# Tile starts at multiples of 64 bytes, deeper buffers in stick-breaking and up-projection, and an output projection begun by contraction block

## The chip, the core and the metric

The kernel runs on one core of one Trainium2 chip. The metric is the device time of one execution in microseconds (us). Times of before are from three runs; a further execution was profiled, and all rows below are of that one.

## What is computed

One decoder layer over 1024 tokens of width 1024, float32 throughout. Two attention families run from one input projection, are projected up, gated and summed, and go through an output projection; then a squared-ReLU MLP. Each half has a shift, a scale and a gate computed from a vector `c` ("ada"). Cut to what matters here:

```python
mod = jax.nn.silu(c) @ ada_w + ada_b
shift1, scale1, gate1, shift2, scale2, gate2 = jnp.split(mod, 6, axis=-1)
z = (rms_norm(h, norm1_g) * (1 + scale1) + shift1) @ w_in
...                                   # q_a, k, v of NSA; q_b, k_b, v_b; m_a, m_b
y_a = nsa_attention(...) @ w_up_nsa   # compressed, selected and sliding-window branches
y_b = stick_breaking_attention(q_b, k_b, v_b) @ w_up_sb
mixed = (jax.nn.sigmoid(m_a) * y_a + jax.nn.sigmoid(m_b) * y_b) @ w_out
h = h + gate1 * mixed
u2 = rms_norm(h, norm2_g) * (1 + scale2) + shift2
ff = jnp.square(jax.nn.relu(u2 @ mlp_w1)) @ mlp_w2
return h + gate2 * ff
```

Stick-breaking has no softmax: with z the scaled logits, the weight of a key is sigmoid(z) times the product of sigmoid(-z) over the later keys up to the query.

## The kernel before, in words

**Matmuls.** Every large product is made of three TensorE (PE) passes: each float32 operand is split into a rounded high half and the rest (tiles ending in `h` and `l`, by `hi` and `lo`, lines 57 to 66), and high by high, high by low and low by high are summed in PSUM. A matmul has a stationary operand of 128x128 and a moving one of up to 512 columns.

**Memory.** Tiles are taken from pools that grow from two ends of the on-chip memory, "left" and "right". The right end begins 32 bytes off a multiple of 64, so with tile sizes that are multiples of 64 a right-hand tile starts at 32 modulo 64; odd-sized tiles (`rows`, `zero` of 4 bytes, `Pt` of 513 elements, `wh1`/`wl1` of 536) shift what lies behind them.

**Stages** (times of the profiled execution): norm and first projections (0 to 185; lines 300, 304, 575, 586), native sparse attention (NSA, 215 to 600), stick-breaking (600 to 857), rest of the input projection (to 880), up-projections (880 to 982), output projection (976 to 1092), MLP (1092 to 1756). The columns of `w_in` for q_b, k_b, v_b and the gates are computed as "fill" (line 744, 24 matmuls for one block of 128 columns and 512 tokens): a generator hands out its matmuls between those of the two attentions. `pump` hands out so many us of it at once: 25 ahead of NSA, 20 between NSA and stick-breaking. What is left at the end runs by itself.

**Order.** The code gives each engine's work; a scheduler orders the instructions of each engine when the kernel is built, and each engine runs its list in that order. DMAs are issued from SyncE's (SP's) list, also in order.

**Ada rows.** `ada_rest` (line 410) computes a row of `c @ ada_w` in steps: a load (`adraw`, two buffers), a multiply on ScalarE (ACT, L439), an add on GpSimd (POOL, L443). Row 3 runs in stick-breaking in pieces of 256 columns, row 0 (the gate of the first half) in the up-projection in pieces of 512. `side(n)` runs n steps.

**Stick-breaking** (`sb_gens`). Per head and group: logits on PE (L1121 to L1124) into a bank `psx`, two sigmoids on ACT (L1126 into a tile `sig128` to `sig512` or `sigr`, L1127 in place), a scan on VectorE (DVE, L1136), a product on POOL (L1138), transposes (L1153), a split (`th`, `tl`), and products with V (L1173). At the start, head 0 is prepared: casts and subtractions to `Q`, `Kh`, `Kl` (ACT, POOL), V by transposes and casts (L1091, L1095).

**Up-projection** (lines 1370 to 1397). 16 units (8 blocks of 128 channels, two token halves) for each branch; a unit is 12 matmuls of L1322, a gate tile `m` loaded and put through a sigmoid, and a product (L1379). Branch 1 runs `lag` units behind branch 0 and the two are summed on POOL (L1394) and split to `mth`/`mtl`. Weights come in units of 256 columns (`w_unit`: load into one of three `raw` buffers, cast on POOL L63, rest on DVE L66).

**Output projection** (`out_mm`). The contraction has 8 blocks in four weight units; a result of 128 tokens and 512 columns is 24 matmuls (L1426).

**MLP.** 64 hidden units of 24 matmuls (L1510) alternate with the products of a Strassen-like scheme (L1559, 24 a product).

## Time and profile before

| | us |
|---|---|
| median of 3 runs | 1753.86 |
| lowest, highest | 1750.43, 1757.51 |
| profiled execution | 1757.71 |
| its span in the trace | 1755.7 |
| PE busy in the span | 1697.4 (97%) |
| DVE, POOL, ACT busy | 1140.2, 872.2, 818.1 |

The profiled execution's time lies 2.0 us above its span, which begins with the first instruction and ends with the last. A matmul's duration in the trace is that of its way through the array and overlaps the next; what a matmul costs in a run is the distance from start to start. The granted clock is TensorE's, as a share of 2.4 GHz; the other level is 1.2 GHz.

### The profile page before, as it was taken

To read this page: it belongs to the slowest core of one execution; us is meant where nothing else is said; L and a number is where in the kernel's file an instruction comes from. 1 tells how busy PE (TensorE), PEld (TensorE's weight loads), DVE (VectorE), ACT (ScalarE), POOL (GpSimd) and SP (SyncE) were. 2 spreads that over 40 slices of the span, in tenths; PEclk is the share of its full clock that TensorE was granted. 3 is DMA by queue.
4 is the path that set the end of the run, shared out by engine and by line. 5 is a ranking of instruction groups with operands and counts; after the bars stand their busy time and mean duration, and the time that the engine had idled before them with its cause. 6 is when DMAs were issued, how large, how long until landed. Compare 5 with 4: busy or idle time off the path is not lost.

```text
span 1755.7 us, 25197 instructions
## 1 busy us (share of the span) xinstructions
PE 1697.4 (97%) x8652; PEld 1417.0 (81%) x8652; DVE 1140.2 (65%) x2514; ACT 818.1 (47%) x1809; POOL 872.2 (50%) x824
## 2 busy tenths in 40 slices
PE   5999999999999989999999899999999999999998
PEld 4879888888888867788778687888888888888886
DVE  7597478778777467778454564365656564756458
ACT  6433476666666367766443244333333333333332
POOL 0021143434333387874154400786867675858676
PEclk8999999999999989999999999999999999999999
DMA  9365312112121254531475611121212020202102
GB/s 300 101 191 153 109 46 60 49 54 60 44 59 39 76 156 129 148 84 46 149 249 174 215 37 72 38 71 37 64 41 76 25 72 25 72 25 72 43 19 96
DMA packets 153655, 157.12 MB, mean 89 GB/s; under 512 B 13544, under 2 KB 117688, under 8 KB 153528
## 3 DMA queue, kind: packets, MB, share of 16 engines
q1 hardware_dynamic: 149304, 153.42, 29.3%
q10 hardware_dynamic: 4224, 2.10, 0.4%
q8 instruction: 68, 1.11, 0.3%
q14 instruction: 59, 0.48, 0.1%
HBM read 128.21 MB, written 27.28 MB: 89 GB/s over the span
## 4 chain that ended last, share of the span: by engine, by line
PE 79%; DMA 6%; DVE 4%; POOL 4%; ACT 3%; issue 3%; SPq 1%; POOLq 0%; ACTq 0%; DVEq 0%
PE px L1510 20%; PE px L1559 16%; PE pd L744 15%; PE px L1426 5%; PE po L907 4%; PE pt L941 4%; DMA adraw<-in_ada_w_dram 3%; PE psx L823 2%; PE psx L824 2%; PE po L1173 1%; PE cb L300 1%; PE pd L586 1%; PE psx L586 1%; PE pt L1153 1%; POOL adacc L443 1%
## 5 line engine op out<-in xcount | busy, mean ns | idle before, releaser
L1562 DVE TENSOR_TENSOR acc<-acc,px 128x512 f32<-128x512 f32 x384 | 244.0, 683 | 121.8 <-PE px L1559 116.5
L1510 PE MATMUL px<-mtl,wh 128*128 128x512 f32 x512 | 203.4, 397 | 0.0
L1510 PE MATMUL px<-mth,wl 128*128 128x512 f32 x512 | 203.3, 397 | 0.0
L1510 PE MATMUL px<-mth,wh 128*128 128x512 f32 x512 | 203.0, 397 | 0.0
L744 PE MATMUL pd<-uh,uwh 128*128 128x512 f32 x448 | 180.7, 403 | 0.7 <-ACT zo L1016 0.7
L744 PE MATMUL pd<-ul,uwh 128*128 128x512 f32 x448 | 177.5, 396 | 0.0
L1559 PE MATMUL px<-wbl,rah 128*128 128x512 f32 x448 | 175.5, 392 | 2.1 <-POOL wbl L1535 1.8
L744 PE MATMUL pd<-uh,uwl 128*128 128x512 f32 x448 | 176.9, 395 | 0.0
L1559 PE MATMUL px<-wbh,ral 128*128 128x512 f32 x448 | 174.7, 390 | 0.0
L66 DVE TENSOR_TENSOR wl<-raw,wh 128x1024 fp32r<-128x1024 f32 x48 | 74.9, 1563 | 150.7 <-ACT wh L61 129.2
L1559 PE MATMUL px<-wbh,rah 128*128 128x512 f32 x448 | 172.5, 391 | 0.0
L1535 POOL TENSOR_TENSOR wbl<-raw,wbh 128x1024 fp32r<-128x1024 f32 x40 | 104.2, 2606 | 93.6 <-ACT wbh L1534 93.4
L1521 POOL TENSOR_TENSOR w<-w,grow 128x1024 f32<-128x1024 f32 x32 | 83.1, 2612 | 98.2 <-DVE grow L1294 97.9
L899 DVE TENSOR_TENSOR tl<-pt,th 128x512 fp32r<-128x512 f32 (+8 forms) x168 | 103.7, 620 | 34.5 <-ACT th L898 33.3
L1533 POOL TENSOR_TENSOR raw<-r 128x512 f32<-128x512 f32 x80 | 109.7, 1392 | 20.2 <-DVE wl L66 18.1
L898 ACT CAST th<-pt 128x512 fp32r<-128x512 f32 (+8 forms) x168 | 88.7, 530 | 60.4 <-PE pt L941 58.4
L1510 PEld LDWEIGHTS px<-mth,wl 128*128 128x128 f32 x512 | 96.5, 189 | 23.6 <-DVE grow L1294 0.2
L1510 PEld LDWEIGHTS px<-mtl,wh 128*128 128x128 f32 x512 | 96.6, 189 | 23.2 <-issue 0.2
L1510 PEld LDWEIGHTS px<-mth,wh 128*128 128x128 f32 x512 | 96.6, 189 | 23.1 <-issue 0.2
L1534 ACT CAST rah<-raw 128x1024 fp32r<-128x1024 f32 x40 | 42.0, 1050 | 152.9 <-PE px L1559 139.6
L1559 PEld LDWEIGHTS px<-wbl,rah 128*128 128x128 f32 x448 | 84.1, 188 | 21.4 <-POOL wbl L1535 3.0
L1559 PEld LDWEIGHTS px<-wbh,rah 128*128 128x128 f32 x448 | 84.1, 188 | 18.4
(322 smaller groups left out, 4548.1 us busy)
## 6 DMA issues: line engine op xcount, KB each, us to landing
raw<-in_mlp_w_dram SPq DMA_DIRECT2D x32, 512.0 KB, 4.1
w<-in_mlp_w_dram SPq DMA_DIRECT2D x32, 512.0 KB, 4.1
z_d<-zo SPq DMA_DIRECT2D x56, 256.0 KB, 2.0
uwr<-in_w_in_dram SPq DMA_DIRECT2D x54, 256.0 KB, 3.0
adraw<-in_ada_w_dram SPq DMA_DIRECT2D x48, 256.0 KB, 2.9
xa<-in_ada_w_dram SPq DMA_DIRECT2D x32, 256.0 KB, 6.1
zr<-z_d SPq DMA_DIRECT2D x32, 256.0 KB, 4.8
m<-z_d SPq DMA_DIRECT2D x32, 256.0 KB, 3.3
```

The lines of the kernel that those rows point to most:

```text
L66: (nc.vector if e == "v" else nc.gpsimd).tensor_tensor(dst, src, f(h), op=OP.subtract)
L744: r = nc.tensor.matmul(p, a, b, start=(k == 0 and n == 0), stop=(k == NK - 1 and n == 2))
L898: nc.scalar.copy(th[:rows, :w], p[:rows, :w])
L899: nc.vector.tensor_tensor(tl[:rows, :w], p[:rows, :w], f(th)[:rows, :w], op=OP.subtract)
L907: track(nc.tensor.matmul(po_[:, :256], w, tt[q][:rows, m * 256:(m + 1) * 256], start=(n == 0 and m == 0 and q == 0), stop=(n == last and m ...
L1426: nc.tensor.matmul(p, a[:, k, ts_], b[:, k % 2], start=(k == 0 and n == 0), stop=(k == NK - 1 and n == 2))
L1510: nc.tensor.matmul(p, a[:, k], b[th][:, k], start=(k == 0 and m == 0), stop=(k == NK - 1 and m == 2))
L1521: nc.gpsimd.tensor_tensor(t, t, grow2, op=OP.mult)
L1533: nc.gpsimd.tensor_tensor(d, block(i0, j0, s), block(i1, j1, s), op=OP.add if sg > 0 else OP.subtract)
L1535: (nc.vector if e == "v" else nc.gpsimd).tensor_tensor(l.rearrange("p s n -> p (s n)"), src, f(h).rearrange("p s n -> p (s n)"), op=OP.sub ...
L1559: nc.tensor.matmul(p, a[:, s, qs], b[:, s], start=(s == 0 and n == 0), stop=(s == 1 and n == 2))
L1562: nc.vector.tensor_tensor(acc[:, t, ds_], acc[:, t, ds_], p, op=OP.add if sg > 0 else OP.subtract)
```

## The change

What it does, in the order of the diff:

- A tile of 32 bytes is put first on the right-hand side, and tiles of odd size are made multiples of 64 bytes (`rows` becomes a part of an `acc` tile, 536 columns become 544, 63-column blocks lie in 512 elements, `zero` takes 16 elements, `Pt` 528). `kv_mm` splits its 536 columns 272 and 264 instead of twice 268.
- Stick-breaking: head 0 is prepared on DVE instead of POOL; three `sig` buffers a width instead of two and six `sigr` instead of five; no ada steps in the first three groups; 24 us of fill instead of 20 ahead of it.
- Up-projection: branch 0's gate tiles get seven buffers instead of five, the lag is 5 instead of 3, and ada row 0 goes in pieces of 256 columns, two steps a unit.
- Output projection: the first four results are begun together, 6 matmuls each from one weight unit, before the next unit.

```diff
+    pool("odd", "right").tile([128, 8], F32, name="odd")
     xt_pool = pool("xt", "right")
...
-        rows = xt_pool.tile([72, 128], F32, name="rows")
+        rows = xt_pool.tile([128, 2, 128], F32, name="acc", bufs=2)[:72, 0]
...
-        wh = p1a.tile([128, 536], F32R, name="wh1", bufs=8)
-        wl = p1a.tile([128, 536], F32R, name="wl1", bufs=8)
+        wh = p1a.tile([128, 544], F32R, name="wh1", bufs=8)
+        wl = p1a.tile([128, 544], F32R, name="wl1", bufs=8)
...
-        for c in range(2):
+        for c, (c0, c1) in enumerate(((0, 272), (272, 536))):
...
-        zero = sp.tile([128, 1], F32, name="zero")
+        zero = sp.tile([128, 16], F32, name="zero")[:, 0:1]
...
+            eng, e = (nc.gpsimd, "g") if h else (nc.vector, "v")
...
-            hi(Kh, kr, "g")
+            hi(Kh, kr, e)
             yield
-            nc.gpsimd.tensor_tensor(Q[HD:], qr[HD:], f(Q)[HD:], op=OP.subtract)
+            eng.tensor_tensor(Q[HD:], qr[HD:], f(Q)[HD:], op=OP.subtract)
...
-            lo(Kl, kr, Kh, "g")
+            lo(Kl, kr, Kh, e)
...
-            sig = sp.tile([128, w], F32, name="sigr" if kind == 1 else "sig%d" % w, bufs=5 if kind == 1 else 2)
+            sig = sp.tile([128, w], F32, name="sigr" if kind == 1 else "sig%d" % w, bufs=6 if kind == 1 else 3)
...
-                Pt = sp.tile([128, 513], F32, name="Pt", bufs=6)
+                Pt = sp.tile([128, 528], F32, name="Pt", bufs=6)
...
-                    if c % 2:
+                    if c % 2 and k > 2:
                         side(1)
...
-        m = pool_.tile([128, 512], F32, name="m%d" % br, bufs=5 - 3 * br)
+        m = pool_.tile([128, 512], F32, name="m%d" % br, bufs=7 - 5 * br)
...
-    pump(fill, 20.0)
+    pump(fill, 24.0)
...
-    ada_steps = ada_rest(yb, (0,), 2, "s")
+    ada_steps = ada_rest(yb, (0,), 2, "s", 256)
     side(1)
-    lag = 3
+    lag = 5
...
-        side(1)
+        side(2)
...
+    def out_part(p, t, dh, ks):
         ts_ = slice((t % 4) * 128, (t % 4 + 1) * 128)
         th = t // 4
-        p = px()
-        for k in range(NK):
+        for k in ks:
             wh, wl = wo_s[dh][k // 2]
...
+    def out_mm(t, dh, p=None):
+        ds_ = slice(dh * 512, (dh + 1) * 512)
+        if p is None:
+            p = px()
+            out_part(p, t, dh, range(NK))
...
+    ob_ = [px() for _ in range(4)]
+    for k in range(0, NK, 2):
+        for t in range(4):
+            out_part(ob_[t], t, 0, (k, k + 1))
     for t in range(4):
-        out_mm(t, 0)
+        out_mm(t, 0, ob_[t])
```

Where the operands of the matmuls start, in the two built programs (line numbers of before; bytes modulo 64 of the moving and of the stationary operand, and the difference of the two modulo 256):

| line | what | count | before: moving, stationary | difference | after: moving, stationary | difference |
|---|---|---|---|---|---|---|
| 300 | first blocks | 96 | 0, 32 | 96 | 0, 0 | 64 |
| 304, 575 | q columns | 192 | 0 or 32, 0 | 0, 32, ... 224 | 0, 0 | 0, 128 |
| 744 | fill | 1344 | 0, 0 | 0 | 0, 0 | 0 |
| 907 | NSA, probabilities by V | 592 | 32, 32 | 0 | 0, 0 | 0 |
| 1121, 1122 | stick-breaking logits | 192 | 32, 32 | 0 | 0, 0 | 0 |
| 1322 | branch 0 | 192 | 32, 32 | 0 | 0, 0 | 0 |
| 1322 | branch 1 | 192 | 0, 32 | 96 | 0, 0 | 64 |
| 1426 | output projection | 384 | 32, 0 | 160 | 0, 0 | 192 |
| 1510 | hidden units | 1536 | 0, 32 | 96 | 0, 0 | 64 |
| 1559 | MLP products | 1344 | 0, 0 | 0 | 0, 0 | 0 |

The order of PE at the start of the output projection. Before: `px_12320`, `px_12349` and `px_12378` are the first three results, `wh_12294`, `wh_12300` and `wh_12306` the high halves of weight units 0, 1 and 2.

```order
L1426 MATMUL px_12349<-wl_12301,mth0_11512 128x512
L1426 MATMUL px_12320<-wh_12306,mth0_11512 128x512
L1426 MATMUL px_12349<-wh_12300,mtl0_11514 128x512
L1426 MATMUL px_12349<-wh_12300,mth0_11512 128x512
L1426 MATMUL px_12349<-wl_12301,mth0_11512 128x512
L1426 MATMUL px_12349<-wh_12300,mtl0_11514 128x512
L1426 MATMUL px_12349<-wh_12306,mth0_11512 128x512
```

Unit 2 was first used after 20 matmuls, by the second row above. After, with `px_12390` to `px_12393` the four results, `wh_12364` unit 0 and `wh_12370` unit 1 (the rows where unit 0 gives way to unit 1):

```order
L1427 MATMUL px_12393<-wh_12364,mth0_11516 128x512
L1427 MATMUL px_12393<-wl_12365,mth0_11516 128x512
L1427 MATMUL px_12393<-wh_12364,mtl0_11518 128x512
L1427 MATMUL px_12390<-wh_12370,mth0_11516 128x512
L1427 MATMUL px_12390<-wl_12371,mth0_11516 128x512
```

Unit 1 is first used after 24 matmuls, unit 2 after 48, unit 3 after 72.

The order of POOL around the casts of these weights (L63), among the sums of the two branches (L1394, L1397 after). Before, from the cast of unit 1 to that of unit 3:

```order
L63 TENSOR_SCALAR wh_12300<-raw_12299 128x1024
L1394 TENSOR_TENSOR m1_12107<-m1_12107,m0_11948 128x512
L1394 TENSOR_TENSOR m1_12148<-m1_12148,m0_12002 128x512
L1394 TENSOR_TENSOR m1_12185<-m1_12185,m0_12043 128x512
L1394 TENSOR_TENSOR m1_12208<-m1_12208,m0_12090 128x512
L63 TENSOR_SCALAR wh_12306<-raw_12305 128x1024
L1394 TENSOR_TENSOR m1_12228<-m1_12228,m0_12131 128x512
L63 TENSOR_SCALAR wh_12312<-raw_12311 128x1024
```

After, the same stretch (`wh_12370` is unit 1, `wh_12376` unit 2):

```order
L63 TENSOR_SCALAR wh_12370<-raw_12369 128x1024
L1397 TENSOR_TENSOR m1_12213<-m1_12213,m0_11947 128x512
L1397 TENSOR_TENSOR m1_12238<-m1_12238,m0_12011 128x512
L1397 TENSOR_TENSOR m1_12258<-m1_12258,m0_12057 128x512
L63 TENSOR_SCALAR wh_12376<-raw_12375 128x1024
L1397 TENSOR_TENSOR m1_12278<-m1_12278,m0_12102 128x512
L63 TENSOR_SCALAR wh_12382<-raw_12381 128x1024
L1397 TENSOR_TENSOR m1_12298<-m1_12298,m0_12147 128x512
```

Unit 2's cast has moved ahead of one more branch sum. On SP, the load of unit 0 stood after branch 1's ninth gate tile and ahead of 13 gate tiles; now it stands after branch 0's sixteenth and branch 1's tenth, ahead of 6.

The order of ACT at the start of stick-breaking. Before (`V` casts of head 0 and 1, `adacc` and `adraw` the ada steps):

```order
L439 ACTIVATE adacc<-adraw,cs 128x256
L439 ACTIVATE adraw<-adraw,cs 128x256
L1073 CAST Q<-zr 128x1024
L439 ACTIVATE adraw<-adraw,cs 128x256
L1095 CAST V<-pt 128x4x64 x2
L439 ACTIVATE adraw<-adraw,cs 128x256
L1095 CAST V<-pt 128x4x64 x2
L1126 ACT_TABLE_LOAD
```

After:

```order
L441 ACTIVATE adacc<-adraw,cs 128x256
L1076 CAST Q<-zr 128x1024
L441 ACTIVATE adraw<-adraw,cs 128x256 x4
L1098 CAST V<-pt 128x4x64 x2
L1018 COPY zo<-pd 128x512
L1098 CAST V<-pt 128x4x64 x2
L1129 ACT_TABLE_LOAD
```

Five ada steps instead of four stand ahead of the first sigmoid, and all five ahead of the V casts. Of the fill, 70 matmuls stood between NSA and the first V transpose and now 89; between each twelve products of L1173 it was 18 to 38 throughout, and now it is 12 to 42 with none in the last such stretch.

## Rows read from the trace of the kernel before

**Rows 1.** The page, busy time, share of the span and instructions by engine.

```profile
PE 1697.4 (97%) x8652; PEld 1417.0 (81%) x8652; DVE 1140.2 (65%) x2514; ACT 818.1 (47%) x1809; POOL 872.2 (50%) x824
```

**Rows 2.** Busy time by stretch: engines as its heading says, then clock, DMA share, GB/s.

```profile
core 0: us, PE busy (x) PEld busy (x) DVE busy (x) ACT busy (x) POOL busy (x), PEclk, DMA share, GB/s
...
600.00:640.00 40.00, 33.73 (x155) 27.54 (x154) 16.61 (x33) 17.62 (x37) 23.44 (x23) 0.91 0.69 187
640.00:860.00 220.00, 208.35 (x1130) 172.95 (x1129) 168.79 (x323) 146.83 (x339) 141.26 (x148) 0.98 0.35 93
...
987.00:1026.00 39.00, 39.00 (x163) 31.30 (x163) 22.80 (x36) 8.76 (x20) 8.21 (x6) 0.94 0.62 216
...
1134.00:1710.00 576.00, 576.00 (x2495) 469.39 (x2494) 345.00 (x425) 192.88 (x263) 411.59 (x233) 1.00 0.16 49
```

**Rows 3.** Chain that ended last: start, length in us, engine, tile, line, matmuls.

```profile
45.11 2.83 PE cb L300 x12
...
85.85 5.34 PE qb L575 x23
...
756.60 2.73 PE pd L744 x12
...
856.69 21.80 PE pd L744 x96
...
1030.88 11.22 PE px L1426 x48
...
1133.92 5.46 PE px L1559 x24
1139.39 5.61 PE px L1510 x24
```

**Rows 4.** Timeline of PE in the up-projection, branch 0, then branch 1: start, us.

```profile
882.67 0.39 PE L1322 MATMUL px<-oh,wh 128*128 128x512 f32 x1
...
884.03 0.39 PE L1322 MATMUL px<-oh,wh 128*128 128x512 f32 x1
...
972.08 0.40 PE L1322 MATMUL px<-ol,wh 128*128 128x512 f32 x1
...
974.42 0.39 PE L1322 MATMUL px<-oh,wl 128*128 128x512 f32 x1
```

**Rows 5.** Timeline of PE, its three longest waits after 600 (in brackets).

```profile
631.95 0.47 PE L1121 MATMUL psx<-Kh,Q 128*128 128x128 f32 x1 [5.40 <-DVE Pt L1136]
...
891.67 0.50 PE L1322 MATMUL px<-oh,wh 128*128 128x512 f32 x1 [2.26 <-POOL wh L63]
...
986.08 0.80 PE L1426 MATMUL px<-wh,mth 128*128 128x512 f32 x1 [4.89 <-POOL wh L63]
```

**Rows 6.** Output weights: unit 0's load in the chain, then SP's and POOL's timelines.

```profile
945.87 8.62 DMA raw<-in_w_out_dram
...
956.97 0.38 SPq L1281 DMA_DIRECT2D raw<-in_w_out_dram  x1
...
971.78 0.38 SPq L1281 DMA_DIRECT2D raw<-in_w_out_dram  x1
...
983.75 1.26 POOL L1394 TENSOR_TENSOR m<-m,m 128x512 f32<-128x512 f32 x1 [3.07 <-DVE m L1379]
984.98 1.05 POOL L63 TENSOR_SCALAR wh<-raw 128x1024 fp32r<-128x1024 f32 x1
```

**Rows 7.** Waits, 632 to 860 (ACT to 857): total us, times, longest.

```profile
ACT sig L1126 <- PE pt L1153: 13.5, 10, 3.2
...
ACT sigr L1126 <- PE pt L1153: 3.9, 7, 0.8
...
PE psx L1121 <- DVE Pt L1136: 11.8, 8, 5.4
```

**Rows 8.** Timeline of ACT at the start of stick-breaking, fourth and fifth ada step.

```profile
627.20 0.51 ACT L439 ACTIVATE adraw<-adraw,cs 128x256 f32<-128x256 f32 x1 [1.36 <-DMA adraw<-in_ada_w_dram]
...
631.81 0.51 ACT L439 ACTIVATE adraw<-adraw,cs 128x256 f32<-128x256 f32 x1 [0.39 <-DMA adraw<-in_ada_w_dram]
```

More of the change, by code (lines that the diff above doesn't have):

```diff
@@ L514, in add @@
             if 0 in hs:
-                blks[g] = cp.tile([128, 4, 2, NCB], F32, name="blk", bufs=2)
+                blks[g] = cp.tile([128, 512], F32, name="blk", bufs=2)[:, :8 * NCB].rearrange("p (j h c) -> p j h c", j=4, h=2)
             for h in hs:
@@ L580, in kv_mm @@
     def kv_mm(t):
-        raw = pb.tile([128, 536], F32, name="kvr", bufs=2)
-        for c in range(2):
+        raw = pb.tile([128, 544], F32, name="kvr", bufs=2)
+        for c, (c0, c1) in enumerate(((0, 272), (272, 536))):
             p = (pd, psx)[c]()
@@ L585, in kv_mm @@
                 for n, (a, b) in enumerate(three(k, slice(t * 128, (t + 1) * 128))):
-                    nc.tensor.matmul(p[:, :268], a, ws[k][b][:, c * 268:(c + 1) * 268],
+                    nc.tensor.matmul(p[:, :c1 - c0], a, ws[k][b][:, c0:c1],
                                      start=(k == 0 and n == 0), stop=(k == NK - 1 and n == 2))
-            nc.scalar.copy(raw[:, c * 268:(c + 1) * 268], p[:, :268])
+            nc.scalar.copy(raw[:, c0:c1], p[:, :c1 - c0])
         return raw
@@ L1416, in build @@
     wo = I["w_out"][0].rearrange("(k p) d -> p k d", p=128)
-    def out_mm(t, dh):
-        ds_ = slice(dh * 512, (dh + 1) * 512)
+    def out_part(p, t, dh, ks):
         ts_ = slice((t % 4) * 128, (t % 4 + 1) * 128)
         th = t // 4
-        p = px()
-        for k in range(NK):
+        for k in ks:
             wh, wl = wo_s[dh][k // 2]
```

## The prediction

> **What bounds the kernel now.** The page comes first: TensorE (PE) is busy in 1697.4 of 1755.7 us [rows 1], so only what shortens PE's own work or its idle time counts, and an engine beside it counts where PE waits for it. The table by stage comes second: the multilayer perceptron (1134 to 1710) keeps PE busy in 576.00 of 576.00 us while POOL, the next, has 411.59; the worst stretches are 600 to 640 (33.73 busy of 40, granted clock 0.91 of full) and stick-breaking, 640 to 860 (208.35 of 220); 987 to 1026 has a clock of 0.94 [rows 2]. Third, the chain that ended last, read for the time of one matmul in unbroken runs [rows 3]. All of these are 128x512 products of the same type, and they fall into two classes: L744 21.80/96 = 227.1 ns and L1559 5.46/24 = 227.5 ns, against L1510 5.61/24 = 233.8 ns and L1426 11.22/48 = 233.8. Fourth, PE's timeline in the up-projection [rows 4]: one line, L1322, has both classes. Branch 0 goes from 882.67 to 884.03 in 6 steps (226.7 ns); branch 1 from 972.08 to 974.42 in 10 (234.0). The table of addresses tells them apart: in both quick lines and in branch 0 the moving and the stationary operand start at the same place modulo 64 bytes, in the slow lines and in branch 1 they differ by 32. Branch 0 has both at 32, so it is not the 32 that costs, but the difference. Fifth, PE's idle times: 5.40 us at 631.95, 2.26 at 891.67 and 4.89 at 986.08 [rows 5].
>
> The Trainium skill, page "TensorE: Matmul & The Clock Gate", section "Wait — 56ns, not 53.3ns?", gives back-to-back matmuls one price, columns over the clock and a fixed rest, 215.7 ns at 512 columns, with no term for an address. The trace has 227 and 234 for one shape, so it disagrees twice; by that rule the first term below would be zero (the rival "no price").
>
> **Part 1, addresses.** Nothing is added to PE's order in the perceptron; every start becomes a multiple of 64. The price of a difference of 32 is 233.8 - 227.1 = 6.7 ns a matmul. Counts from the loops: L1510 has 64 units of 24 = 1536, so 10.3 us; L1426 16 tiles of 24 = 384, 2.6 us; branch 1 of L1322 16 units of 12 = 192, 1.3 us. The first products: L300 takes 2.83/12 = 235.8, so 96 x 8.7 = 0.8 us; L575 and L304 alternate equal and unequal starts, 5.34/23 = 232.2, so 192 x 5.1 = 1.0. L744 in short runs between other products shows 2.73/12 = 227.5, 0.4 ns over the long run; for some 1,000 such with their neighbours I take 1 us, an estimate. Sum 17.0. All of it is on the path: PE has no idle time in the perceptron for the saving to fall into, and what follows (the last 46 us, where POOL has its part) starts that much earlier. Bounds if the rule holds: 14.2 (the three lines with plain rows) to 20. The 268-column products split 272/264 keep their columns: 0.
>
> What the rows do not show: every quick stretch above has a difference that is a multiple of 256. After the change L744 and L1559 keep that, but the hidden units have 64, the output projection 192, branch 1 64. Single matmuls with 64, 128 and 192 exist (three eighths of L575), but only between others, and the line's mean of 232.2 [rows 3] shows neither class. So "64 is enough" is the assumption, and two rivals hang on it.
>
> **Part 2, output projection begun with the contraction outermost.** Before, PE runs 20 of these matmuls and then needs the third weight unit's high half: 4.89 us idle at 986.08 for POOL's wh [rows 5]. That cast ran at 984.98, behind the branch sum of 983.75 in POOL's order, and its load was issued at 971.78, since three units share one staging buffer (loads at 945.87, 956.97, 971.78); a load alone took 8.62 us [rows 6]. After the wait PE stood at the lower clock level (1.2 GHz of 2.4): 39.0 us at 0.94 is 39 x 0.06 = 2.3 us lost [rows 2]. Wait and clock together are 7.2 us, the most that can be gained. After, each unit feeds 24 matmuls = 5.5 us, so unit 2 is needed 11 us after the start and not 4.7; in POOL's order its cast stands ahead of two branch sums instead of one. Against that, unit 0 is loaded later: in the new order it follows the load of the sixteenth gate tile of branch 0, which with seven buffers waits for the ninth branch sum. Then 9 units of 12 x 0.227 = 2.7 us are left on PE, 24.6 us, less some 2.5 for a result's way over DVE and POOL (the sum alone 1.26): the load is some 22 us ahead of the projection, where it was 31 (from 945.87 to 986.08 - 4.89 - 20 x 0.234 = 976.5). From unit 0's load to unit 2's cast it was 984.98 - 945.87 = 39 us; with the first round's 956.97 - 945.87 = 11.1 twice, a load and nothing to wait for, it is 2 x 11.1 + 8.6 = 31. So unit 2 is cast 9 to 17 us after the start, and is needed at 11: a wait of 0 to 6 stays. I take 1.5 us with little clock lost, near the lower end since POOL's order has the cast earlier. Gain 5 (0 to 7). The four results then leave together, which costs nothing as long as PE has the next tile's 24 matmuls (5.5 us) and four other banks to go on with; without them it would be the two DVE operations that each result takes now.
>
> **Part 3, up-projection.** Seven buffers, lag 5, and the second modulation row's steps halved to 256 columns, two a unit. PE here waits once, 2.26 us at 891.67 for the cast of branch 1's first weight [rows 5]. The longer lag should take it away, but in PE's order branch 1's first unit still comes after four units of branch 0, as before: 0. Two more gate loads stand ahead of that weight's load on SP's queue (up to 1.5 us worse); if it vanishes, 4 with the clock. Halved steps double the count of loads; they end up on the way to unit 0's load and are priced in part 2.
>
> **Part 4, stick-breaking.** Third sigmoid buffers: ScalarE (ACT) waited 13.5 us in 10 places for PE to free a "sig" and 3.9 in 7 for a "sigr", and PE in turn 11.8 us for DVE's scans, of which 5.40 is the opening [rows 7]. A part of the remaining 6.4 goes: 3. The opening: ACT starts its sigmoids behind the V casts and four modulation steps, the fourth at 627.20 after 1.36 us of waiting for its load; the fifth comes at 631.81 [rows 8]. The change means these steps to start later, but in the new order of ACT five of them stand ahead of the V casts. So the first sigmoid follows a step like that of 631.81 instead of that of 627.20: 631.81 - 627.20 = 4.6 later, against 19 more fill matmuls (24 us pumped instead of 20), 19 x 0.227 = 4.3 us of work done meanwhile. Net 0.3 worse, with the casts after it 1.5. The fill used there is missing at the end: the last stretch of stick-breaking has none, where each stretch before had 18 to 36 matmuls; PE waits there like at other bare places, 1 to 2 us. Sum 3 - 1.5 - 1.5 = 0, bounds -6 (a whole second opening wait) to +6 (all the 6.4).
>
> **Sum.** 17 + 5 + 0 + 0 = 22 us against the profiled run of 1757.7 (span 1755.7 and 2.0 around it): 1735.7. That run lies 3.9 above the median 1753.9, so the forecast for a median is 1732.
>
> **The rivals.**
> "256, not 64": only differences that are multiples of 256 are fast. For: every long quick stretch has one. Against: 6.7 ns are 16 clock cycles whether the difference is 96 (L1510, L300) or 160 (L1426), so nothing grows with the distance. Then part 1 gives nothing: 1732 + 17 = 1749.
> "No price": addresses do not set the two classes, and something else in these stages does. Against: L1322 in one stage with both. Also 1749. (The rule from the Trainium skill above would have it so.)
> "The wait moves": unit 2 and with it the clock are as late as before: part 2 gives 0, 1737.
> "The opening grows": the five modulation steps ahead of the V casts follow their loads at the 4.6 us that lie between the fourth and the fifth now, not only once, and the clock stays low after it: part 4 at -6, 1738. For it: ACT waits for just these loads [rows 8].
> "Other offsets cost more": the one that ends slower. Differences of 64 and 192 could cost more than those of 32. Place: L300, hidden units, output projection, branch 1, 2208 matmuls. Price: if 13.4 ns instead of 6.7, they cost 29.6 us where they now cost 15.0 (8.7 x 96 among them), 14.6 more, and part 2 takes off 5: 1763.5. It decides from (15.0 + 5)/2208 = 9.1 ns on, a hidden-unit matmul of 236 ns. Nothing in the trace shows such a step; against it stands L575, a quarter of whose matmuls have such differences and whose mean is 232.2.
>
> **How the numbers follow.** About 0.5% (8.8 us) is what a measurement of this kernel can tell from no change: faster is under 1745.1, slower over 1762.6. Chances: forecast 0.58, "the wait moves" 0.12, "the opening grows" 0.09 (all three faster); "256" 0.12, "no price" 0.03 (both the same); "other offsets" 0.06 (slower). So 0.79, 0.15, 0.06. Time 1732. The forecast's own range, with part 1 at 14 to 20, part 2 at 0 to 7, part 4 at -6 to +6 and the 3.5 us by which the runs scatter, is 1722 to 1743; to leave out no more than 2 in 10, the range goes to 1747, into the two cases at 1749, and down to 1721.
>
> **What would show it.** Right: in the chain, hidden units at 227 to 228 ns (5.46 for 24), as their neighbours; the output projection the same; the perceptron's stage 10 us shorter; PE's idle time ahead of the third weight unit under 3 us and the stretch after it at clock 0.98 or more. Wrong in part 1: hidden units at 233.8. Wrong in part 2: a gap of 4 us or more in the first 24 matmuls that use unit 2, and again a low clock. Part 4: the idle time at the first scan, near 5.4, and fewer waits of sigmoids on the transposes; if PE's idle time in stick-breaking (220 - 208.35 = 11.65 us) falls under 6, I was too low there. The forecast as a whole is wrong if the sum of the stages outside the perceptron loses more than 5 us.

## The result and the profile after

| | before | after |
|---|---|---|
| median, us (runs) | 1753.78 (6) | 1766.91 (6) |
| lowest, highest | 1748.18, 1757.51 | 1764.68, 1770.32 |
| profiled execution, its span | 1757.71, 1755.7 | 1770.32, 1768.6 |

The changed kernel takes 1.0069 times as long, 95% interval 1.0055 to 1.0083: it is slower by 13 us, where the forecast had it 22 us faster. Line numbers of after lie 2 to 12 higher: hidden units are L1522, the MLP's products L1571, the output projection L1427, the up-projections L1325, the sum of the branches L1397, an ada step L441.

First the page's busy times and the table by stage, to be held against [rows 1, 2] (the columns are the same).

```profile
PE 1699.4 (96%) x8652; PEld 1417.7 (80%) x8652; DVE 1136.7 (64%) x2517; ACT 822.7 (47%) x1825; POOL 870.9 (49%) x835
```

```profile
600.00:640.00 40.00, 33.10 (x161) 27.19 (x159) 12.51 (x26) 11.19 (x21) 14.79 (x13) 0.95 0.66 174
640.00:860.00 220.00, 204.22 (x1096) 169.49 (x1097) 166.02 (x329) 150.22 (x350) 145.69 (x154) 0.97 0.34 94
...
987.00:1026.00 39.00, 32.55 (x128) 25.16 (x127) 24.94 (x26) 8.69 (x17) 15.57 (x12) 0.94 0.70 242
1134.00:1710.00 576.00, 576.00 (x2498) 468.93 (x2497) 346.56 (x422) 196.16 (x266) 417.63 (x235) 1.00 0.16 49
```

PE is not less busy than before, and stick-breaking and the opening of the output projection have more idle time: 15.8 us of 220 where it was 11.65, and 6.5 of 39 (before's 4.89 lay just ahead of that stretch). The MLP's 576 us hold 2498 matmuls where they held 2495, so it has hardly become quicker. The chain of after (start, length, engine, tile, line, matmuls) says why, against [rows 3]:

```profile
43.94 2.81 PE cb L302 x12
...
1044.37 11.00 PE px L1427 x48
...
1146.46 5.45 PE px L1571 x24
1151.91 5.60 PE px L1522 x24
```

A hidden unit still takes 5.60/24 = 233.3 ns a matmul beside products at 5.45/24 = 227.1. Only the output projection moved, from 233.8 to 11.00/48 = 229.2. PE's timeline shows the waits (in brackets, with what ended them) that stand where [rows 5] stood:

```profile
641.15 0.47 PE L1124 MATMUL psx<-Kh,Q 128*128 128x128 f32 x1 [7.37 <-DVE Pt L1139]
...
900.79 0.50 PE L1325 MATMUL px<-oh,wh 128*128 128x512 f32 x1 [2.50 <-POOL wh L63]
902.57 0.79 PE L1325 MATMUL px<-oh,wl 128*128 128x512 f32 x1 [1.05 <-DVE wl L66]
...
991.71 0.50 PE L1427 MATMUL px<-wh,mth 128*128 128x512 f32 x1 [0.81 <-DVE m L1382]
996.41 0.50 PE L1427 MATMUL px<-wh,mth 128*128 128x512 f32 x1 [3.04 <-DVE m L1382]
1024.23 0.75 PE L1427 MATMUL px<-wh,mth 128*128 128x512 f32 x2 [2.59 <-POOL wh L63]
```

The table below is made from the starts of the first matmuls of each stage on PE in the two traces (the last row ends with the start of the last matmul). It shows where the 13 us of the profiled pair lie.

| stretch on PE | before | after | difference |
|---|---|---|---|
| start of the trace to the first long fill | 185.3 | 188.5 | +3.2 |
| from there to the first logits of stick-breaking | 437.9 | 442.1 | +4.2 |
| first logits to the end of the opening wait | 8.8 | 10.6 | +1.7 |
| end of the opening wait to the up-projection | 246.4 | 246.1 | -0.3 |
| up-projection | 97.7 | 100.4 | +2.7 |
| output projection and norm, to the first hidden unit | 103.9 | 105.0 | +1.1 |
| MLP, first hidden unit to last product | 671.7 | 672.0 | +0.3 |

The 3.2 us of the first row are one wait of 2.66 us at 156.34 and a lower clock behind it. It is absent in the run with the address edits alone, where this stage is the same, and 0.50 us in that of the whole change with a 96-byte tile, whose first row is 184.0 us; so it belongs to this execution. The 4.2 us are the 19 fill matmuls that were put ahead of stick-breaking; they would be nothing if stick-breaking ended earlier for it, and it does not. The 2.7 us of the up-projection are less than the change costs there, since before's own trace is a slow one at this place: its granted clock is 0.94 from 874 to 902, where three of the runs below that leave this part as it was (the output projection's and the stick-breaking edits alone, the third buffers alone) have 1.00 and take 95.3 to 95.7 us for the up-projection. Against these after loses some 5 us.

### The profile page after: what moved, and what is told of

The parts are those of the page before. It is cut to its first block, busy times and chain, and to the rows that moved or that the text cites. A ratio compares the mean times of both kernels' runs of the same rounds, so it can differ in the third digit from the quotient of the medians.

```text
span 1768.6 us, 25255 instructions
## 1 busy us (share of the span) xinstructions
PE 1699.4 (96%) x8652; PEld 1417.7 (80%) x8652; DVE 1136.7 (64%) x2517; ACT 822.7 (47%) x1825; POOL 870.9 (49%) x835
## 4 chain that ended last, share of the span: by engine, by line
PE 78%; DMA 6%; DVE 5%; POOL 5%; ACT 3%; issue 2%; SPq 1%; POOLq 0%; DVEq 0%; ACTq 0%
PE px L1522 20%; PE px L1571 16%; PE pd L746 14%; PE po L909 4%; PE px L1325 4%; PE pt L943 4%; PE px L1427 4%; DMA adraw<-in_ada_w_dram 2%; PE psx L825 2%; PE psx L826 2%; DMA raw<-in_w_out_dram 1%; PE cb L302 1%; POOL raw L1545 1%; PE po L1176 1%; PE pt L1156 1%
## 5 line engine op out<-in xcount | busy, mean ns | idle before, releaser
L1522 PE MATMUL px<-mtl,wh 128*128 128x512 f32 x512 | 202.9, 396 | 0.0
L1522 PE MATMUL px<-mth,wl 128*128 128x512 f32 x512 | 202.7, 396 | 0.0
L1522 PE MATMUL px<-mth,wh 128*128 128x512 f32 x512 | 202.5, 396 | 0.0
L1571 PE MATMUL px<-wbl,rah 128*128 128x512 f32 x448 | 175.3, 391 | 3.2 <-POOL wbl L1547 2.9
L1571 PE MATMUL px<-wbh,ral 128*128 128x512 f32 x448 | 174.9, 390 | 0.0
L1571 PE MATMUL px<-wbh,rah 128*128 128x512 f32 x448 | 172.2, 390 | 0.0
L1522 PEld LDWEIGHTS px<-mth,wl 128*128 128x128 f32 x512 | 96.2, 188 | 23.6 <-issue 0.2
L1522 PEld LDWEIGHTS px<-mtl,wh 128*128 128x128 f32 x512 | 96.2, 188 | 23.1 <-issue 0.2
L1522 PEld LDWEIGHTS px<-mth,wh 128*128 128x128 f32 x512 | 96.2, 188 | 22.9 <-issue 0.2
L1571 PEld LDWEIGHTS px<-wbl,rah 128*128 128x128 f32 x448 | 84.1, 188 | 23.1 <-POOL wbl L1547 4.2
L746 PEld LDWEIGHTS pd<-uh,uwl 128*128 128x128 f32 x448 | 84.7, 189 | 18.4
```

Source lines behind the costliest of these rows:

```text
L746: r = nc.tensor.matmul(p, a, b, start=(k == 0 and n == 0), stop=(k == NK - 1 and n == 2))
L1522: nc.tensor.matmul(p, a[:, k], b[th][:, k], start=(k == 0 and m == 0), stop=(k == NK - 1 and m == 2))
L1571: nc.tensor.matmul(p, a[:, s, qs], b[:, s], start=(s == 0 and n == 0), stop=(s == 1 and n == 2))
```

## Experiments: addresses

The theory on record said that a difference of the two operands' starts that is a multiple of 64 bytes is fast; the rival said 256. Before has its right-hand tiles at 32 bytes off, so one tile of another size ahead of all others shifts every right-hand tile and leaves the order of all engines as it was:

```diff
+    pool("odd", "right").tile([128, N], F32, name="odd")   N = 88, 24, 56
```

With 352 bytes, the mixed lines (first blocks, branch 1, output projection, hidden units) differ by multiples of 512; with 96 bytes by odd multiples of 256; with 224 bytes by 128 modulo 256.

> The kernel before, with one tile of 352 bytes put first on the right-hand side of the memory and nothing else; every engine's order stays as it was. The starts of the moving and the stationary operand of the hidden units, the output projection, branch 1 and the first blocks then differ by a multiple of 512. Theory A (a matmul is quick where the two starts differ by a multiple of 512): all of these at 227 ns a matmul, 5.45 us for 24, about 14 to 17 us off the median, near 1738. Theory B (256 is enough): the same here. Theory C (it is the side of the memory that counts: quick where both operands lie on the same side): nothing moves, hidden units at 233.8, near 1754.

> The same with a tile of 96 bytes: the starts differ by 256 modulo 512. Theory A: hidden units stay at 233 to 234 ns, near 1754. Theory B: 227 ns, near 1738. Theory C: 233.8, near 1754.

> The same with a tile of 224 bytes: the starts differ by 128 modulo 512 (by 384 in the output projection), all starts are multiples of 64. Theories A and B: 233 to 234 ns, near 1753, as in the changed kernel where they differ by 64. A theory that 128 is enough: 227 ns, near 1738. Theory C: 233.8, near 1754.

The fourth run has the change's address edits alone (the 32-byte tile and all the tile sizes), the fifth the whole change with one number altered:

```diff
-    pool("odd", "right").tile([128, 8], F32, name="odd")
+    pool("odd", "right").tile([128, 24], F32, name="odd")
```

> The address edits of the change alone: the 32-byte tile, the rounded tile sizes and the split into 272 and 264 columns. My prediction's part 1 had 17 us for it, near 1737. After the result: hidden units at 233.3 as in the changed kernel, output projection near 229, the wait of 2.66 us before the compressed keys' transpose (line 568 of the changed kernel) with the low clock behind it also here if it comes from the addresses and column split by way of the scheduler; then near 1754 to 1757. If that wait does not appear here, near 1751.

> The changed kernel with its tile of 32 bytes made 96, so that the starts which differed by 64 or 192 differ by 256; nothing else moves. If the address rule found is right (256 is enough, 64 is not): hidden units, branch 1 and output projection at 227 ns, 10.0 + 1.2 + 0.9 us off, 1754 to 1755, level with the kernel before. If the changed kernel's loss were itself due to addresses, it would fall to near 1738.

The medians, and the mean distance from start to start of back-to-back 128x512 matmuls, ns (distances over 300 ns are left out; each ratio is to the runs of before that were taken with that kernel, with medians of 1753.78 to 1754.74):

| kernel | median, us | ratio to before, 95% | hidden units | output projection | difference modulo 256: hidden, output |
|---|---|---|---|---|---|
| before | 1754.74 | | 234.1 | 233.7 | 96, 160 |
| 352-byte tile | 1741.12 | 0.9911 to 0.9942 | 226.7 | 227.2 | 0, 0 |
| 96-byte tile | 1739.22 | 0.9899 to 0.9932 | 226.7 | 227.3 | 0, 0 |
| 224-byte tile | 1748.92 | 0.9959 to 0.9983 | 232.6 | 232.5 | 128, 128 |
| address edits of the change | 1753.57 | 0.9983 to 1.0004 | 233.4 | 229.0 | 64, 192 |
| after | 1766.91 | 1.0055 to 1.0083 | 233.4 | 229.3 | 64, 192 |
| after, tile of 96 bytes | 1752.69 | 0.9975 to 1.0001 | 226.7 | 227.5 | 0, 0 |

The chain of the kernel with the 96-byte tile (here hidden units are L1511, products L1560):

```profile
1025.72 10.90 PE px L1427 x48
...
1126.27 5.44 PE px L1560 x24
1131.71 5.44 PE px L1511 x24
```

The chain of the kernel with the 224-byte tile, the same places:

```profile
1025.86 11.20 PE px L1427 x48
...
1128.35 5.45 PE px L1560 x24
1133.79 5.59 PE px L1511 x24
```

With a multiple of 256 a hidden unit is as quick as the product beside it, 5.44 and 5.44; with 128 it is not. So the address is the cause, and 256 is the step: 64, 96, 128 and 160 all lie at 232.5 to 234.1, 192 at 229. That it is the difference and not the place of one operand is seen in the up-projection. Branch 0 has both operands on the right-hand side, so that the added tile moves them together: its second, third and fourth unit take 226.6 or 226.7 ns a matmul in all seven kernels. Branch 1 has one operand on each side, and its last units take 234.0 to 234.5 ns in before, 233.3 in after, 233.7 to 233.9 with the 224-byte tile and 226.6 to 226.7 with those of 96 and 352.

One tile of 96 bytes is worth 15.5 us, and the distances account for it: 1536 x 7.4 ns (hidden units), 384 x 6.4 (output projection) and 192 x 7.7 (branch 1) are 15.3 us. The MLP, from the first hidden unit to the last product, takes 659.5 us with it where it took 671.7. The 224-byte tile did better than was expected of it: it is 5.8 us under before (3.0 to 7.2 by the interval), of which the distances explain some 3; what the rest is stays open. Alone, the change's own address edits are worth 1.2 us, with an interval that holds zero. In the changed kernel the 96-byte tile is worth 1766.91 - 1752.69 = 14.2 us. The rest of the change costs just as much whichever way the addresses lie: 1766.91 - 1753.57 = 13.3 us beside its own address edits, 1752.69 - 1739.22 = 13.5 beside the 96-byte tile.

The Trainium skill, page "TensorE: Matmul & The Clock Gate", section "Wait — 56ns, not 53.3ns?", has one price for back-to-back matmuls of 512 columns, 215.7 ns, without an address in it. The runs disagree on both: 226.7 and 234.1 for one shape in one stage.

## Experiments: the three other parts alone

Each is the kernel before with one part of the diff that stands with the change, word for word: the output projection begun with the contraction outermost; the up-projection (seven buffers, lag 5, ada row 0 in halved steps, two a unit); stick-breaking (preparation on DVE, third buffers, later ada steps, 24 us of fill).

> The kernel before with the output projection's edit alone (four results begun together by weight unit). The prediction's part 2: the wait of 4.89 us for the third unit's cast goes, 5 us off (0 to 7), near 1749.5. Rival from the trace of the changed kernel (banks): four results at once need four PSUM banks, and the last up-projection units still hold theirs until DVE has read them; then the first 24 matmuls stop for DVE's product of the up-projection (line 1379), two stops of 1 to 3 us each with the low clock behind them, and the gain is eaten up: 1753 to 1756.

> The kernel before with the up-projection's edits alone (seven gate buffers, lag 5, the ada row in 32 steps of 256 columns, two a unit). The prediction's part 3 had nothing for it (-1.5 to +4). Rival: the 32 steps and the longer lag put the first output weight's load behind them on SP's list, some 14 us ahead of the output projection instead of 30; then the third unit's cast comes later, the wait of 4.89 us grows to 12 to 20 us, near 1764. In between if only the up-projection's own waits grow (2.26 to 3.55 us, with the low clock 2.7 us longer): near 1757.

> The kernel before with the stick-breaking edits alone (head 0 prepared on DVE, third sigmoid buffers, no ada steps in the first three groups, 24 us of fill ahead). The prediction's part 4: 0 (-6 to +6). From the trace of the changed kernel: from the first logits to the start of the 96 last fill matmuls 235 us there against 233.6, and 4.3 us more fill ahead, so 5.7 us slower, near 1760; the opening wait 7.4 us instead of 5.4.

| part alone | median, us | ratio to before (1754.56), 95% | difference |
|---|---|---|---|
| output projection | 1755.64 | 0.9999 to 1.0025 | +1.1 |
| up-projection | 1762.55 | 1.0030 to 1.0061 | +8.0 |
| stick-breaking | 1762.99 | 1.0030 to 1.0061 | +8.4 |

With the addresses, -1.2 + 1.1 + 8.0 + 8.4 = 16.3 against 13.1 of the whole, 3 us apart. The four intervals together leave about 5 us open either way, so whether the parts overlap at all is not shown.

**Output projection.** PE's timeline in the run with this part alone:

```profile
986.35 0.50 PE L1424 MATMUL px<-wl,mth 128*128 128x512 f32 x1 [0.86 <-DVE wl L66]
1005.00 0.79 PE L1424 MATMUL px<-wh,mth 128*128 128x512 f32 x1 [3.68 <-POOL wh L63]
```

The wait of 4.89 us for unit 2 is gone, as the change means it to, and 3.68 us stand 19 us later, ahead of the 113th matmul, at the third weight unit of the second half of the columns. POOL's timeline shows what that unit's cast waited for:

```profile
1003.90 1.04 POOL L63 TENSOR_SCALAR wh<-raw 128x1024 fp32r<-128x1024 f32 x1 [10.54 <-DMA raw<-in_w_out_dram]
```

In before the same cast came at 1006.70, 30.7 us after the projection's first matmul against 30.4 here. The edit leaves this load where it was, so PE, which is no longer held at unit 2, runs up against it. The rival on record for this run, a wait for banks, does not occur in it; it does in after (the two waits for L1382 above, at the first matmuls of the third and the fourth result).

**Up-projection.** SP's timeline has unit 0's load at 964.39, against 945.87 of before [rows 6], and PE's projection begins at 977.33: 13 us ahead, where it was 30. PE then waits in the first 22 us of the projection for 1.82, 4.95 and 0.66 us and two shorter times, and the clock of 976 to 1030 is 0.91 where before has 0.94. To see which of the three edits does it, the halved steps alone:

```diff
-    ada_steps = ada_rest(yb, (0,), 2, "s")
+    ada_steps = ada_rest(yb, (0,), 2, "s", 256)
...
-        side(1)
+        side(2)
```

> The kernel before with only the ada row of the up-projection in 32 steps of 256 columns, two a unit (lag 3, five gate buffers). If the 8 us that the up-projection's edits cost come from the halved steps delaying the output weights' loads: near 1760 to 1763, the third unit's wait grown to 10 us or more. If they come from the lag of 5 with seven buffers: 1754 to 1756.

It gave 1760.79 us, 1.0042 [1.0027, 1.0057], 6.1 above before: three quarters of the part. The expected mark, a wait of 10 us or more for unit 2, did not appear. But the row is done later and the weights behind it too, as SP's timeline of that run shows (start, us, line, what):

```profile
960.22 0.38 SPq L1281 DMA_DIRECT2D raw<-in_w_out_dram  x1
970.56 0.38 SPq L1281 DMA_DIRECT2D raw<-in_w_out_dram  x1
976.84 0.38 SPq L1281 DMA_DIRECT2D raw<-in_w_out_dram  x1
```

Unit 0 is loaded 14.4 us later than before, and PE waits for units 1 and 2:

```profile
975.61 0.76 PE L1426 MATMUL px<-wh,mth 128*128 128x512 f32 x1 [2.70 <-POOL wh L63]
...
987.19 0.80 PE L1426 MATMUL px<-wh,mth 128*128 128x512 f32 x1 [4.47 <-POOL wh L63]
```

With a third wait of 0.50 us these are 7.7 us in place of 4.89, and the granted clock of the 59 us from the start of the projection on is 0.88 where before has 0.94: from its first matmul to the first hidden unit it takes 109.6 us instead of 103.9. The rest of the part's loss shows in the up-projection itself, which takes 95.8 us here and 100.6 with the whole part: there PE waits 2.77 and 1.05 us for branch 1's first weights, and the clock of 874 to 902 is 0.88 against 1.00 here. Whether the lag or the gate buffers do that was not separated.

**Stick-breaking.** The third buffers alone, then the longer fill alone, then everything but the longer fill (on the kernel with the 96-byte tile):

```diff
-            sig = ... bufs=5 if kind == 1 else 2)
+            sig = ... bufs=6 if kind == 1 else 3)
```

> The kernel before with the third sigmoid buffers alone. The prediction had 3 us off for it, near 1751.5. From the traces of the stick-breaking edits: ScalarE's waits for a buffer fall from 13.5 to about 3 us, and waits for PE's logits come in their place: no change, 1753 to 1756.

```diff
-    pump(fill, 20.0)
+    pump(fill, 24.0)
```

> The kernel before with one number changed: 24 us of fill ahead of stick-breaking instead of 20. Theory (the longer fill is what puts all ada steps ahead of the first sigmoid): in ACT's order five ada steps now stand ahead of head 0's V casts, as in the run with the stick-breaking edits alone, although the edit that means those steps to start later is absent. PE's wait at the first scan is 7 to 8 us instead of 5.4, and the kernel is 5 to 9 us above before (1759 to 1763). Rival (the later steps and the preparation on DVE carry the loss): the fill only fills, the wait is 5.4 less some part of the 4.3 us of added fill, and the time is before's within 2 us.

> The kernel with the 96-byte tile (1739.2) plus the stick-breaking edits of the change without the longer fill: preparation of head 0 on DVE, third sigmoid buffers, no ada steps in the first three groups, fill at 20 us. In ACT's order three ada steps stand ahead of the first sigmoid instead of four (five with 24 us of fill). Theory (the ada steps ahead of the first sigmoid set the opening wait): the wait at the first scan falls from about 5 us to 1 to 3, and the time is 1733 to 1737. Rival (the other two edits carry the loss that the stick-breaking edits brought): the time is 1743 to 1748, 4 to 9 above.

The third buffers gave 1754.94 us, 0.9998 [0.9989, 1.0007]: nothing. The waits of that run, over the stretches of [rows 7], are as expected:

```profile
ACT sig L1126 <- PE psx L1122: 20.2, 17, 3.1
...
ACT sig L1126 <- PE pt L1153: 0.7, 3, 0.3
...
PE psx L1121 <- DVE Pt L1136: 9.8, 10, 5.7
```

ACT no longer waits for a free "sig" (0.7 us instead of 13.5), but for PE's logits in its place (20.2 instead of 5.1), and PE's waits for the scans go from 11.8 to 9.8 without a gain in the total.

The longer fill alone gave 1762.22, 1.0043 [1.0031, 1.0055]: 7.6 of the 8.4 us. ACT's timeline in that run (in brackets: idle before, and what ended it), then PE's:

```profile
628.99 0.51 ACT L439 ACTIVATE adraw<-adraw,cs 128x256 f32<-128x256 f32 x1 [1.98 <-POOL adacc L443]
633.30 1.04 ACT L439 ACTIVATE adraw<-adraw,cs 128x256 f32<-128x256 f32 x2 [3.80 <-DMA adraw<-in_ada_w_dram]
634.25 0.63 ACT L1095 CAST V<-pt 128x256 fp32r<-128x256 f32 x2
...
635.93 1.28 ACT L1126 ACT_TABLE_LOAD   x1
637.22 0.60 ACT L1126 ACTIVATE sig<-psx 128x512 f32<-128x512 f32 x1
```

```profile
639.62 0.47 PE L1121 MATMUL psx<-Kh,Q 128*128 128x128 f32 x1 [7.54 <-DVE Pt L1136]
```

The edit that wants the steps later is not in this kernel, and still six ada steps, where before has four, stand ahead of the V casts and the first sigmoid: the longer fill alone brings that order about. ACT stands 3.80 us for a load, its first sigmoid comes at 637.22 where before had it at 629.55, and PE resumes 2.40 us behind it. In before, in after, in the run of the whole part and in these three that distance is 2.40 us, and from there to the up-projection it is 245.0 to 248.4 us, whether 70 or 89 fill matmuls were done ahead. So the time of the first sigmoid decides, and fill done early is not regained.

The last of the three gave 1742.19 us, 0.9939 [0.9923, 0.9954], 3.0 above the 96-byte tile alone with intervals that overlap, and the theory's 1733 to 1737 was missed. Only three steps stand ahead of the first sigmoid, but the third waits for a load too, and the opening wait is 6.43 us where the 96-byte tile alone had 4.70:

```profile
626.91 0.51 ACT L440 ACTIVATE adraw<-adraw,cs 128x256 f32<-128x256 f32 x1 [3.43 <-DMA adraw<-in_ada_w_dram]
```

So it is not the number of the steps that counts, but when the load of the last of them lands.

## Experiments: what would gain

All of these stand on the kernel with the 96-byte tile (1739.22). They test the two waits that the change went for.

Output weights loaded earlier: the four units are asked for ahead of the gate row instead of behind it.

```diff
+    wo_s = {0: [w_unit(...) for k in range(4)]}      # ahead of gate_row
```

> The 96-byte tile, and the first four output weights loaded ahead of the gate row instead of behind it. Theory (the wait for the third weight unit comes from its late load, three units taking turns in one staging buffer while the gate row holds the other two): the wait of 6.8 us at the start of the output projection goes, and the low clock behind it: 1730 to 1733 against 1739. Rival (banks, as in the changed kernel: the first results wait for banks that DVE has yet to read): a wait of 2 to 4 us stays, near 1736.

1737.99 us, 0.9912 [0.9897, 0.9927]: the same as the 96-byte tile. Unit 2 was loaded at 942.50, 26 us earlier than with the tile alone (968.38), and its cast comes only 1.3 us earlier (981.49 there). PE's wait of 6.82 us is still 5.01 and not gone, as POOL's timeline and PE's show:

```profile
978.93 1.26 POOL L1395 TENSOR_TENSOR m<-m,m 128x512 f32<-128x512 f32 x1 [3.02 <-DVE m L1380]
980.16 1.05 POOL L63 TENSOR_SCALAR wh<-raw 128x1024 fp32r<-128x1024 f32 x1
```

```profile
981.26 0.80 PE L1428 MATMUL px<-wh,mth 128*128 128x512 f32 x1 [5.01 <-POOL wh L63]
```

The late load was therefore not what held unit 2. Its cast stands behind a branch sum that waits for the last units of branch 1, and, by the code, it goes into one of three weight buffers that branch 1's last unit still holds. With the cast put into other buffers:

```diff
-    ... *((wx, 3) if k < 3 else ())) for k in range(4)]
+    ... *((wx, 3) if k < 2 else ())) for k in range(4)]
```

> The 96-byte tile, and the third output weight unit's two halves put into the buffers that the fourth uses instead of those that branch 1's weights hold. Theory (the third unit's cast can't run before branch 1's last matmul, because it writes the buffer of branch 1's last weight, and then stands behind branch sums in POOL's order): the cast moves ahead, the wait of 6.8 us at the start of the output projection goes, with the low clock after it: 1731 to 1734 against 1739 of the tile alone. If a wait of the same length appears at the fourth unit or at the next four weights, 1737 to 1740.

1740.60 us, 0.9928 [0.9909, 0.9947]: the cast comes earlier (974.84, which is 8.3 us after the projection's first matmul instead of 10.9), the single wait becomes 1.00, 3.44, 0.47 and 1.38 us, the last of them for the sums' own split (ACT `mth` L61), and the total is unchanged. The theory's 1731 to 1734 was missed.

Ada row 3 taken out of stick-breaking, once into the output projection, once into NSA, one step a unit:

```diff
-    ada_steps = ada_rest(sp, (3,), 2, "s", 256)
+    ada_steps = iter(())
...
+    ada_steps = ada_rest(t4, (3,), 2, "s", 256)    # output projection: side(5) a result
...
+    ada_steps = ada_rest(wu, (3,), 2, "s", 256)    # NSA instead: side(1) a unit
```

> The 96-byte tile, and ada row 3 computed in the output projection instead of in stick-breaking, so that no ada load or step can stand ahead of the first sigmoids. Theory (the opening of stick-breaking is ScalarE standing in order behind ada steps that wait for their loads): the opening wait of 4.7 us shrinks to 1 to 3, the sigmoids start 2 to 4 us earlier, stick-breaking ends 3 to 6 us earlier: near 1735 against the 1739 of the tile alone. Rival (the opening waits for the loads of q, k and v and the casts after them, which come no earlier): the same wait, 1738 to 1740.

> The 96-byte tile, and ada row 3 computed during native sparse attention, one step a unit, instead of in stick-breaking or (as in ada3late) in the output projection. Theory (stick-breaking's opening waits for ada loads in ScalarE's order): the opening wait is under 1.5 us and the clock stays up, as in ada3late, and nothing is lost later: 1731 to 1734 against 1739. Rival (the steps cost native sparse attention what they save): 1737 to 1741, that stage 3 to 6 us longer.

In the output projection: 1745.57 us, 0.9942 [0.9918, 0.9965]. PE's wait at the opening falls to 0.89 us and the up-projection starts 6.2 us earlier than with the 96-byte tile, but the output projection waits 8.74 us for unit 2 and 3.65 more at 1020.46, and takes 115.0 us to the first hidden unit where the tile alone has 102.9:

```profile
627.84 0.33 PE L1122 MATMUL psx<-Kh,Q 128*128 128x128 f32 x1 [0.89 <-DVE Pt L1137]
...
978.32 0.79 PE L1427 MATMUL px<-wh,mth 128*128 128x512 f32 x1 [8.74 <-POOL wh L63]
```

In NSA: 1748.08 us, 0.9965 [0.9952, 0.9978]. The opening wait is gone too, but stick-breaking starts at 637.82 instead of 622.38; PE is busy in 403.51 of the 415 us from 185 to 600 where the 96-byte tile alone has 411.45. So the steps cost that stage more than they save, and more than the rival had put on it. Two combinations followed: this with unit 2's other buffers, and that with third sigmoid buffers as well.

> Both of these on the 96-byte tile: 1725 to 1729 if the two waits are independent; the opening wait under 1.5 us, the wait for the third unit gone.

> The same with the ada row in native sparse attention and the third sigmoid buffers: if the buffers bring nothing because stick-breaking waits for PE's logits and not for buffers, as sbsig says, level with best2 (1725 to 1729); if they bring something once the opening is out of the way, 2 to 4 us less.

They gave 1748.02 (0.9962 [0.9950, 0.9974]) and 1744.66 us (0.9944 [0.9928, 0.9960]). Both are far from the 1725 to 1729 that was expected. With the opening free the third buffers may be worth 3.4 us, where on before they were worth nothing; the two intervals overlap, so this is not shown. No version beats the 96-byte tile by more than the runs scatter: that tile, alone, is the best kernel found, 15 us under before and 28 under after.

## Why the prediction was wrong

**What bounds the kernel** held: PE's own time and its waits gave all that was found.

**Part 1** failed at the step that it named itself, the assumption that a multiple of 64 is enough. The rival "256, not 64" occurred and had been given 0.12. The evidence was in the prediction: every quick stretch had a multiple of 256, and no row showed 64, 128 or 192 fast. The term of 17 was 1.2. Where the condition is met the gain is 14.2 us in after and 13.6 and 15.5 us in before, near the lower of the bounds 14.2 to 20: the three lines with plain rows account for 15.3, and the 2.8 us put on the first products and the fill are not seen. "No price" and "other offsets cost more" both fell, the first by the three tiles of other sizes, the second since 64, 128 and 192 cost no more than 96.

**Part 2** was right that unit 2's wait goes (4.89 to under 1 us in the run of the part alone), and wrong that 5 us come of it: +1.1 instead. One step that failed is the assumption that no other wait takes its place. With the part alone 3.68 us come up behind, for the second half's third weight unit, whose load the edit does not move. In after a different bound shows, which the prediction had excluded with "four other banks to go on with": PE waits 0.81 and 3.04 us for DVE's L1382, the operation that reads out the last up-projection results. Four results begun together want four banks at once, and the last ones are still unread. Unit 2's cause was mistaken too: I put it to its load, 39 us from load to cast; the run with the load 26 us earlier shows that it is mostly the place in POOL's order and the buffer: the cast came 1.3 us earlier. In after unit 2 was cast at 997.70, 10.1 us after the start and within the 9 to 17 forecast, and PE did not wait for it. The lead of unit 0's load, forecast at 22 us, was 14 in after, from this SP row to the first matmul at 987.58:

```profile
973.23 0.39 SPq L1284 DMA_DIRECT2D raw<-in_w_out_dram  x1
```

**Part 3** was mis-sized: 0 forecast, +8.0 measured, of which the halved steps are 6.1. The mechanism was named ("they end up on the way to unit 0's load") and then priced at nothing, because it was folded into the lead of a load. Twice as many loads of one queue, each waited for in turn, are a chain of their own: its last step came 15 us later (the last store of the row at 957.52 instead of 942.49). The longer lag did not take away branch 1's first wait (2.50 us in after, 2.26 before), as forecast; a second of 1.05 us and a lower clock came to it, which the prediction did not have.

**Part 4** was forecast at 0 within -6 to +6, and alone it costs 8.4, outside the bounds. The rival "the opening grows" has the right cause, the ada steps ahead of the V casts, and was priced at 6. The delay itself was sized right: counted from the first long fill, the first sigmoid comes 6.0 us later in after and 6.3 with the longer fill alone, and 4.6 and 1.2 had been forecast. What failed is the set-off: 4.3 us of fill done meanwhile was counted as gained, and PE needs it nowhere, since stick-breaking takes as long without it. The prediction also put the five steps' new order to the edit that moves them; the longer fill alone makes it. And of the third buffers' 3 us nothing came, though ACT's waits for a free "sig" fell from 13.5 to 0.7 us [rows 7]: they had not been what held PE.

**The sum.** 17 + 5 + 0 + 0 was forecast; alone the parts measured 1.2 - 1.1 - 8.0 - 8.4, the first two with intervals that hold zero. The rival that had the kernel end slower (other offsets cost more) was not what made it slower. Outside the MLP 12.6 us of the profiled pair were lost, against the 5 that the prediction allowed itself. The slowdown came from two terms that I had set to zero because each had a reason to go either way, and I allowed no case in which both are losses.

## What to carry to other kernels

Before adding padding, check the difference of the two operands' starts against the finest step that the quick rows show, and not a coarser guess. An edit that only makes a chain of loads finer, or moves work ahead of a stage that is bound by a chain on another engine, is not free because the busy engine has something to do; look at when the first instruction of that chain can start. Moving a wait is not removing it: unit 2's wait was taken away in two ways, by PE's order and by the buffers, and the total stayed as it was.

## What the runs showed of the hardware

The time of a back-to-back 128x512 float32 matmul depends on the difference of the SBUF starts of its two operands modulo 256 bytes: 226.6 to 227.5 ns at 0, 229.0 to 229.3 at 192 (the output projection alone), 232.5 and 232.6 at 128 (up to 233.9 in branch 1), 233.3 and 233.4 at 64, 233.7 at 160, 234.0 to 234.5 at 96. Whether the difference is an even or an odd multiple of 256 makes none (226.7 both). I had expected that alignment of each tile to 64 bytes is what counts; with it, the hidden units gained 0.7 ns of the 7.4 that the 96-byte tile gains. Why the array should be quicker at one distance than at another no run here shows.
